# An issue-order edge that keeps a row gather behind the weight splits on VectorE

## Chip, cores and metric

The kernel runs on 1 core of one Trainium2 chip. The metric is the device time of one execution in microseconds. Before the change the median of 3 runs is 3570.77 us (3566.84 to 3582.67 us).

## What is computed

The reference runs two transformer blocks, of depth 2 each, on 256 tokens of width 1024. The change concerns the second block, in which a stream of 256 latent tokens and a stream of 256 context tokens each pass a "PEER" layer: for every token 8 heads choose 16 of 16384 experts, each expert being one row of a table u and one row of a table v.

```
def peer_block(hb, w_q, sub_keys, u_tab, v_tab):
    ...
    expert = jnp.take_along_axis(cand_i, pos, axis=-1)
    g = jax.nn.softmax(top_s, axis=-1)
    u = u_tab[expert]
    act = jax.nn.gelu(jnp.einsum('nhkd,nd->nhk', u, hb).astype(jnp.float32))
    w = (g * act).astype(hb.dtype)
    return jnp.einsum('nhk,nhkd->nd', w, v_tab[expert])
```

## The kernel before, in words

The kernel does not look up rows for most tokens. In its dense form, 448 columns (256 latent tokens, 192 context tokens) go through all 128 slabs of the tables. `ahead` (L1145) computes `hidden` (L1128) for each slab: a 128x1024 piece of u is loaded, split into a high and a low part, multiplied on PE (24 matmuls of 448 columns), put through a GELU and kept in DRAM. `experts` (L1168) then loads each kept slab, weighs it by the routing matrix and multiplies it with a split piece of v. Each split (`split`, L208) is a copy on ACT (L210) and a subtraction on DVE (L211); PE needs both parts. The routing matrix is made beside `ahead`: `choose` (L975) finds the top 16 (DVE, L945 to L949), and `spread` (L1067) builds one-hot tiles (three compares on POOL and one on DVE at L1078, two products on DVE at L1082), multiplies them on PE (L1096) and stores them.

The first 64 context tokens are left out of the dense form. For them `gather` (L1312) fetches the chosen rows: 64 fetches of u rows and 64 of v rows, each 128 rows of 1024 numbers, by an indirect DMA issued on POOL (L1328). Each fetch has one DVE instruction: a product with a sum for u (L1337), a multiply-add for v (L1343; the first one is L1341). There are three landing places, so fetch i+2 needs DVE instruction i-1 to be done. The accumulated result goes to DRAM at the end (L1346, on SP's queue). Two of the three landing places are one tile of the pool "k8", which also holds the split pieces of v.

The source paces this work. `aside` (L1349) ends with `gather` and is a Python generator; each `next` of it traces one fetch and one DVE instruction. Beside the qkv, attention and output projection of the latent stream it is advanced by `beside`. In `ahead` it gets the rate `GP[0]` = 0.22 per unit, and a slab of 448 columns counts two units, so 0.44 gathers per slab. In `experts` it gets `GP[1]` = 0.4 per slab. But the order in which instructions are traced is not the order of the queues: a scheduler sets each engine's queue, and takes first what is ready first.

Of the kernel before, what the change touches and what calls it, by code (L numbers as in the profile page):

```python
# [10 lines left out]
F32 = mybir.dt.float32  # L11
# [3 lines left out]
AF = mybir.ActivationFunctionType  # L15
ALU = mybir.AluOpType
AX = mybir.AxisListType

P = 128
S = 256  # L20
D = 1024
# [37 lines left out]
class Net:  # L59
# [148 lines left out]
    def split(self, hi, lo, src):  # L208

        self.nc.scalar.copy(hi, src)  # L210
        self.nc.vector.tensor_sub(lo, src, hi.bitcast(F32))  # L211

    def cut_in_two(self, shape, raw):

# [1097 lines left out]
    def gather(self, idx, g):  # L1312

        nc, io = self.nc, self.io
        tables = io["u_rows"], io["v"][0].rearrange("a b d -> (a b) d")
        hr, two = self.t("b8", [P, 2, D]), self.t("k8", [P, 2, D])
        h = acc = hr[:, 0]
        places = hr[:, 1], two[:, 0], two[:, 1]  # L1320
        act = self.t("act", [P, P // 2], bufs=1)
        n = P // 2
        for i in range(2):
            nc.sync.dma_start(h[NG * i:NG * i + NG], self.hrd)

        def fetch(i):
            if i < 2 * n:
                nc.gpsimd.indirect_dma_start(out=places[i % 3], out_offset=None, in_=tables[i // n],  # L1328
                                             in_offset=bass.IndirectOffsetOnAxis(ap=idx[:, i % n:i % n + 1], axis=0))

        fetch(0), fetch(1)
        for i in range(2 * n):
            fetch(i + 2)
            r, a = places[i % 3], act[:, i % n:i % n + 1]
            if i < n:
                junk = self.t("b2", [P, D], mybir.dt.bfloat16)
                nc.vector.scalar_tensor_tensor(junk, r, 1.0, h, ALU.mult, ALU.mult, accum_out=a)  # L1337
            elif i == n:
                nc.scalar.activation(act, act, AF.Gelu_apprx_tanh)
                nc.vector.tensor_mul(act, act, g)  # L1340
                nc.vector.tensor_scalar(acc, r, act[:, 0:1], None, ALU.mult)  # L1341
            else:
                nc.vector.scalar_tensor_tensor(acc, r, a, acc, ALU.mult, ALU.add)  # L1343
            yield
        self.accd = self.dr.tile([P, D], F32, tag="accd", name="accd")
        nc.sync.dma_start(self.accd, acc)  # L1346
        yield
# [216 lines left out]
```

## Time and profile before

| | |
|---|---|
| median of 3 runs | 3570.77 us (3566.84 to 3582.67) |
| the profiled execution's own time | 3571.39 us |
| its span in the profile | 3569.5 us |
| mean granted clock of TensorE | 0.974 of full speed |
| busy: PE, DVE, ACT, POOL | 94%, 69%, 42%, 21% of the span |

The stages that the text speaks of, by the time since the span's start: output projection and normalisation of the latent stream about 1110 to 1140 us, key scores from about 1140 us, `ahead` to about 1950 us, `experts` to about 2550 us. The busy share is an average over all stages, so each stage has to be read by itself. In the profile L12 is line 12 of the kernel; a helper's line stands for all its callers, so the weight splits of every stage are L210 and L211. PE executes its queue in order, and so does DVE: an instruction that waits holds back all behind it.

### The profile page before, as it was taken

To read this page: it belongs to the slowest core of one execution; us is meant where nothing else is said; L and a number is where in the kernel's file an instruction comes from. 1 tells how busy PE (TensorE), PEld (TensorE's weight loads), DVE (VectorE), ACT (ScalarE), POOL (GpSimd) and SP (SyncE) were. 2 spreads that over 40 slices of the span, in tenths; PEclk is the share of its full clock that TensorE was granted. 3 is DMA by queue.
4 is the path that set the end of the run, shared out by engine and by line. 5 is a ranking of instruction groups with operands and counts; after the bars stand their busy time and mean duration, and the time that the engine had idled before them with its cause. 6 is when DMAs were issued, how large, how long until landed. Compare 5 with 4: busy or idle time off the path is not lost. (4 is left out here: it accounts for less than half of the span.)

```text
span 3569.5 us, 53463 instructions
## 1 busy us (share of the span) xinstructions
PE 3365.9 (94%) x19488; PEld 2926.8 (82%) x19488; DVE 2445.3 (69%) x5239; ACT 1491.6 (42%) x2523; POOL 743.0 (21%) x728
## 2 busy tenths in 40 slices
PE   8999998999868888899999999999989999999999
PEld 6687867788747867788888999898968999998877
DVE  6657857556878877766666765555467888766665
ACT  6543445444434422233334332333254545555443
POOL 0000001000043476644464000000010046730000
PEclk9999999999988999999999999999999999999999
DMA  7446554344566787754568987787322667788985
GB/s 241 158 159 224 200 168 150 100 153 148 171 204 224 262 272 263 263 186 177 189 219 282 302 266 235 245 256 220 105 67 97 198 239 261 255 287 284 299 277 190
DMA packets 333912, 758.08 MB, mean 212 GB/s; under 512 B 29840, under 2 KB 187920, under 8 KB 327760
## 3 DMA queue, kind: packets, MB, share of 16 engines
q1 hardware_dynamic: 315216, 687.55, 57.3%
q0 software_dynamic: 18432, 67.12, 5.5%
q8 instruction: 153, 2.51, 0.3%
q14 instruction: 111, 0.91, 0.1%
HBM read 659.59 MB, written 94.96 MB: 211 GB/s over the span
## 5 line engine op out<-in xcount | busy, mean ns | idle before, releaser
L210 ACT CAST ws<-w 128x1024 fp32r<-128x1024 f32 (+1 forms) x528 | 547.3, 1037 | 1005.1 <-PE psA L245 728.7
L211 DVE TENSOR_TENSOR ws<-w,ws 128x1024 fp32r<-128x1024 f32 (+1 forms) x528 | 636.6, 1206 | 276.7 <-ACT ws L210 273.7
L246 PE MATMUL psA<-b,ws 128*128 128x256 f32 (+1 forms) x2048 | 669.9, 327 | 50.3 <-DVE ws L211 50.0
L244 PE MATMUL psA<-b,ws 128*128 128x256 f32 (+1 forms) x2048 | 678.5, 331 | 0.0
L1078 POOL TENSOR_SCALAR wb<-iota,R 128x128 f16<-128x128 f16 x528 | 520.6, 1000 | 705.9 <-ACT R L1049 402.7
L245 PE MATMUL psA<-b,ws 128*128 128x256 f32 (+1 forms) x2048 | 665.6, 325 | 0.0
L246 PEld LDWEIGHTS psA<-b,ws 128*128 128x128 f32 x2048 | 390.3, 191 | 78.3 <-DVE ws L211 61.3
L210 ACT CAST k<-wb 128x1024 fp32r<-128x1024 f32 x256 | 268.5, 1051 | 423.8 <-DMA wb<-in_v 423.6
L245 PE MATMUL psC<-k,k 128*128 128x512 f32 (+1 forms) x1056 | 404.9, 384 | 6.1 <-DVE k L211 5.7
L244 PE MATMUL psC<-k,k 128*128 128x512 f32 (+1 forms) x1056 | 402.7, 382 | 6.5 <-ACT k L210 6.5
L246 PE MATMUL psC<-k,k 128*128 128x512 f32 (+1 forms) x1056 | 403.2, 382 | 2.2 <-DVE k L211 2.1
L244 PEld LDWEIGHTS psA<-b,ws 128*128 128x128 f32 x2048 | 392.0, 191 | 15.3
L245 PEld LDWEIGHTS psA<-b,ws 128*128 128x128 f32 x2048 | 390.1, 190 | 15.4
L211 DVE TENSOR_TENSOR k<-wb,k 128x1024 fp32r<-128x1024 f32 x256 | 312.2, 1220 | 68.0 <-ACT k L210 61.5
L159 POOL TENSOR_TENSOR rsrf<-rsvf,neghalf 128x1 f32<-128x1 f32 (+5 forms) x38 | 42.0, 1111 | 1265.8 <-DVE rsvf L158 1264.5
L245 PE MATMUL psC<-ws,k 128*128 128x512 f32 (+1 forms) x608 | 244.0, 401 | 18.0 <-DVE ws L211 17.9
L244 PE MATMUL psC<-ws,k 128*128 128x512 f32 (+1 forms) x608 | 242.0, 403 | 6.6 <-ACT ws L210 5.1
L1191 DVE TENSOR_TENSOR k<-k,b 128x256 f32<-128x256 f32 (+2 forms) x264 | 132.4, 511 | 168.6 <-DMA k<-kept 164.2
L246 PE MATMUL psC<-ws,k 128*128 128x512 f32 (+1 forms) x608 | 241.5, 398 | 0.0
L245 PEld LDWEIGHTS psC<-k,k 128*128 128x128 f32 x1056 | 199.7, 189 | 39.2 <-DVE k L211 8.4
L244 PEld LDWEIGHTS psC<-k,k 128*128 128x128 f32 x1056 | 199.0, 189 | 39.5 <-ACT k L210 7.1
L246 PEld LDWEIGHTS psC<-k,k 128*128 128x128 f32 x1056 | 199.7, 189 | 37.1 <-DVE k L211 5.5
(446 smaller groups left out, 6375.7 us busy)
## 6 DMA issues: line engine op xcount, KB each, us to landing
w<-in_u SPq DMA_DIRECT2D x256, 512.0 KB
wb<-in_v SPq DMA_DIRECT2D x256, 512.0 KB
w<-in_w_ff SPq DMA_DIRECT2D x128, 512.0 KB
G<-k SPq DMA_DIRECT2D x44, 1024.0 KB
wb<-in_ada_w SPq DMA_DIRECT2D x80, 512.0 KB
k<-kept SPq DMA_DIRECT2D x128, 224.0 KB
b<-G SPq DMA_DIRECT2D x15, 1792.0 KB
kept<-k SPq DMA_DIRECT2D x118, 224.0 KB
```

Of the source, the lines that this page charges most:

```text
L159: nc.gpsimd.tensor_tensor(r[:m, :cols], v[:m, :cols], self.neghalf[:m, :cols], op=ALU.pow)
L210: self.nc.scalar.copy(hi, src)
L211: self.nc.vector.tensor_sub(lo, src, hi.bitcast(F32))
L244: self.nc.tensor.matmul(out, ah, bh, start=first, stop=False)
L245: self.nc.tensor.matmul(out, ah, bl, start=False, stop=False)
L246: self.nc.tensor.matmul(out, al, bh, start=False, stop=last)
L1078: eng.tensor_scalar(first[:, j], self.iota16, r0[:, n + j:n + j + 1], None, ALU.is_equal)
L1191: nc.vector.tensor_mul(g3[:, a:b], g3[:, a:b], t[:, :, j])
```

## The change

`split` remembers its DVE subtraction in `self.mark`, and the DVE instructions of one gather step are traced inside `issue_after(self.mark)`. That context gives each DVE instruction in it an ordering edge to the marked one: it is queued behind it on DVE. It is an order of issue alone, with no semaphore. Instructions of other engines are not bound, so neither the indirect DMA on POOL nor the GELU on ACT is.

```
     def split(self, hi, lo, src):
 
         self.nc.scalar.copy(hi, src)
-        self.nc.vector.tensor_sub(lo, src, hi.bitcast(F32))
+        self.mark = self.nc.vector.tensor_sub(lo, src, hi.bitcast(F32)).ins
...
             r, a = places[i % 3], act[:, i % n:i % n + 1]
-            if i < n:
-                junk = self.t("b2", [P, D], mybir.dt.bfloat16)
-                nc.vector.scalar_tensor_tensor(junk, r, 1.0, h, ALU.mult, ALU.mult, accum_out=a)
-            elif i == n:
-                nc.scalar.activation(act, act, AF.Gelu_apprx_tanh)
-                nc.vector.tensor_mul(act, act, g)
-                nc.vector.tensor_scalar(acc, r, act[:, 0:1], None, ALU.mult)
-            else:
-                nc.vector.scalar_tensor_tensor(acc, r, a, acc, ALU.mult, ALU.add)
+            with self.tc.issue_after(self.mark):
+                if i < n:
+                    junk = self.t("b2", [P, D], mybir.dt.bfloat16)
+                    nc.vector.scalar_tensor_tensor(junk, r, 1.0, h, ALU.mult, ALU.mult, accum_out=a)
+                elif i == n:
+                    nc.scalar.activation(act, act, AF.Gelu_apprx_tanh)
+                    nc.vector.tensor_mul(act, act, g)
+                    nc.vector.tensor_scalar(acc, r, act[:, 0:1], None, ALU.mult)
+                else:
+                    nc.vector.scalar_tensor_tensor(acc, r, a, acc, ALU.mult, ALU.add)
```

In the changed kernel the gather's lines are L1338, L1342 and L1344.

Counted over DVE's queue: of the 128 gather instructions, the first 33 stay where they were, give or take some twenty places. Before, the other 95 stand in the normalisation, the key scores and the first third of `ahead`. Now 54 of them stand in `ahead`, 2 or 3 to every 6 weight splits, and 41 in `experts`. The splits, the top-16 search and the one-hots keep their order among one another. Three places follow.

First, DVE's queue in the normalisation after the latent stream's output projection (L174, L158 and L176 are its steps, L941 adds the projection to x, L198 follows PE's transposes), before:

```order
L158 TENSOR_SCALAR rsvf_9979<-nssf_9972 128x1
L1337 SCALAR_TENSOR_TENSOR b_2108_11237,act_8916<-k_1650_8915,b_1649_8914 128x1024
L941 TENSOR_TENSOR x<-x,k_1912_9969 128x512
L176 TENSOR_SCALAR k_1914_9973<-x,rsrf_9980 128x1024
L1337 SCALAR_TENSOR_TENSOR b_2131_11398,act_8916<-b_1649_8914 128x1024
L174 TENSOR_TENSOR nssf_9972<-nssf_9972 128x1
L1337 SCALAR_TENSOR_TENSOR b_2147_11511,act_8916<-k_1650_8915,b_1649_8914 128x1024
L158 TENSOR_SCALAR rsvf_9985<-nssf_9972 128x1
L1337 SCALAR_TENSOR_TENSOR b_2164_11627,act_8916<-k_1650_8915,b_1649_8914 128x1024
L176 TENSOR_SCALAR k_1914_9973<-x,rsrf_9986 128x1024
L1337 SCALAR_TENSOR_TENSOR b_2177_11721,act_8916<-b_1649_8914 128x1024
L198 TENSOR_SCALAR k_1920_9995<-psA_9990,mod_495 128x256
```

And now:

```order
L158 TENSOR_SCALAR rsvf_9979<-nssf_9972 128x1
L941 TENSOR_TENSOR x<-x,k_1912_9969 128x512
L176 TENSOR_SCALAR k_1914_9973<-x,rsrf_9980 128x1024
L174 TENSOR_TENSOR nssf_9972<-nssf_9972 128x1
L158 TENSOR_SCALAR rsvf_9985<-nssf_9972 128x1
L176 TENSOR_SCALAR k_1914_9973<-x,rsrf_9986 128x1024
L198 TENSOR_SCALAR k_1920_9995<-psA_9990,mod_495 128x256
```

The gather instructions between the steps are gone from there.

Second, DVE's queue in `ahead`, at the split whose low part is `ws_12323` (`ws<-w,ws` are the splits of u, `k<-...` at L947 to L949 the top-16 search), before:

```order
L1343 SCALAR_TENSOR_TENSOR b_1649_8914<-k_1650_8915,act_8916,b_1649_8914 128x1024 x2
L947 MATCH_REPLACE k_2254_12237<-k_2235_12128,k_1931_10042 128x128
L211 TENSOR_TENSOR ws_12323<-w_12320,ws_12322 128x1024
L948 MAX k_2235_12128<-k_2254_12237 128x8
L1078 TENSOR_SCALAR wb_12363<-iota_225,R_2239_12145 128x128
L949 MAX_INDEX k_2235_12128<-k_2235_12128,k_2254_12237 128x8
L1082 TENSOR_TENSOR wb_12363<-iota_227,R_12144 128x512
L1343 SCALAR_TENSOR_TENSOR b_1649_8914<-b_1649_8914,act_8916 128x1024
L1082 TENSOR_TENSOR wb_12363<-wb_12363,R_12144 128x512 x2
L1343 SCALAR_TENSOR_TENSOR b_1649_8914<-k_1650_8915,act_8916,b_1649_8914 128x1024
L947 MATCH_REPLACE k_2263_12296<-k_2235_12128,k_1931_10042 128x128
L211 TENSOR_TENSOR ws_12390<-w_12387,ws_12389 128x1024
```

And now:

```order
L947 MATCH_REPLACE k_2254_12237<-k_2235_12128,k_1931_10042 128x128
L211 TENSOR_TENSOR ws_12323<-w_12320,ws_12322 128x1024
L948 MAX k_2235_12128<-k_2254_12237 128x8
L1338 SCALAR_TENSOR_TENSOR b_2271_12355,act_8916<-k_1650_8915,b_1649_8914 128x1024
L949 MAX_INDEX k_2235_12128<-k_2235_12128,k_2254_12237 128x8
L1082 TENSOR_TENSOR wb_12363<-wb_12363,R_12144 128x512 x2
L1078 TENSOR_SCALAR wb_12427<-iota_225,R_2239_12145 128x128
L1082 TENSOR_TENSOR wb_12427<-iota_227,R_12144 128x512
L947 MATCH_REPLACE k_2263_12296<-k_2235_12128,k_1931_10042 128x128
L211 TENSOR_TENSOR ws_12390<-w_12387,ws_12389 128x1024
```

Two gather instructions stood between these two splits and two more before the first; now one stands there, and the next comes two splits later.

Third, DVE's queue in `experts` near the gather's end (`k<-wb,k` is a split of v, `k<-k,k` at L211 a split of the weighed slab, L1191 the weighing), before:

```order
L1191 TENSOR_TENSOR k_3619_21828<-k_3619_21828,b_3590_21577 128x448
L211 TENSOR_TENSOR k_3602_21659<-k_3599_21651,k_3602_21659 128x448
L211 TENSOR_TENSOR k_3609_21726<-wb_21724,k_3609_21726 128x1024
L211 TENSOR_TENSOR k_3606_21695<-k_3603_21687,k_3606_21695 128x448
L211 TENSOR_TENSOR k_3613_21761<-wb_21759,k_3613_21761 128x1024
```

And now:

```order
L1191 TENSOR_TENSOR k_3619_21828<-k_3619_21828,b_3590_21577 128x448
L211 TENSOR_TENSOR k_3602_21659<-k_3599_21651,k_3602_21659 128x448
L1344 SCALAR_TENSOR_TENSOR b_1649_8914<-b_1649_8914,act_8916 128x1024
L211 TENSOR_TENSOR k_3605_21691<-wb_21689,k_3605_21691 128x1024
L211 TENSOR_TENSOR k_3606_21695<-k_3603_21687,k_3606_21695 128x448
L211 TENSOR_TENSOR k_3609_21726<-wb_21724,k_3609_21726 128x1024
```

There was no gather here before. While the gather lives, the split of v (`k_3609`) also stands one slab later against the split of the weighed slab (`k_3606`) than it did.

## Rows read from the trace of the kernel before

**Rows 1.** The page, parts 1 and 3: busy engines; the queue of the indirect DMAs.
```profile
PE 3365.9 (94%) x19488; PEld 2926.8 (82%) x19488; DVE 2445.3 (69%) x5239; ACT 1491.6 (42%) x2523; POOL 743.0 (21%) x728
...
q0 software_dynamic: 18432, 67.12, 5.5%
```
**Rows 2.** Windows by stage: length; busy us of PE, PEld, DVE, ACT, POOL; clock; DMA, GB/s.
```profile
1110.00:1140.00 30.00, 18.63 (x81) 15.21 (x81) 25.64 (x46) 9.61 (x19) 12.84 (x11) 0.73 0.84 298
1140.00:1240.00 100.00, 89.88 (x671) 85.71 (x670) 83.53 (x249) 40.71 (x70) 37.15 (x25) 0.94 0.71 243
1240.00:1500.00 260.00, 218.72 (x1162) 188.98 (x1161) 207.00 (x470) 74.26 (x114) 178.49 (x154) 0.93 0.79 270
1500.00:1800.00 300.00, 300.00 (x1727) 267.68 (x1725) 191.58 (x552) 113.07 (x170) 129.41 (x138) 1.00 0.52 187
1800.00:1950.00 150.00, 145.77 (x877) 129.17 (x876) 96.60 (x193) 60.26 (x92) 94.91 (x96) 0.99 0.73 250
1950.00:2550.00 600.00, 590.82 (x2870) 539.93 (x2871) 360.57 (x514) 191.76 (x250) 0.00 (x0) 0.99 0.77 247
```
**Rows 3.** Windows of L211 alone: DVE busy (weight splits), clock, DMA.
```profile
1240.00:1500.00 260.00, 46.64 (x38) 0.93 0.79 270
1500.00:1800.00 300.00, 68.04 (x56) 1.00 0.52 187
```
**Rows 4.** Waits of PE, 1240 to 1500 us: total, times, longest.
```profile
PE psA L246 <- DVE ws L211: 41.4, 18, 6.8
```
**Rows 5.** Waits of DVE, 1240 to 1500 us.
```profile
DVE b L1343 <- DMA k<-in_v,idx: 27.1, 18, 4.3
DVE b L1343 <- DMA b<-in_v,idx: 22.4, 9, 5.0
```
**Rows 6.** Windows of L1343 alone: DVE busy in the gather.
```profile
1240.00:1500.00 260.00, 81.85 (x63) 0.93 0.79 270
```
**Rows 7.** Timeline of DVE at one stall in `ahead`: start, us, instruction, idle before.
```profile
1401.52 1.28 DVE L1343 SCALAR_TENSOR_TENSOR b<-b,act 128x1024 f32<-128x1024 f32 x1 [4.14 <-DMA b<-in_v,idx]
...
1405.09 1.22 DVE L211 TENSOR_TENSOR ws<-w,ws 128x1024 fp32r<-128x1024 f32 x1
```
**Rows 8.** Timeline of PE at the same stall.
```profile
1406.36 0.74 PE L246 MATMUL psA<-b,ws 128*128 128x448 f32 x1 [3.29 <-DVE ws L211]
1406.90 0.57 PE L244 MATMUL psA<-b,ws 128*128 128x448 f32 x1
1407.27 0.57 PE L245 MATMUL psA<-b,ws 128*128 128x448 f32 x1
...
1412.57 0.37 PE L245 MATMUL psA<-b,ws 128*128 128x448 f32 x1
1412.78 0.37 PE L246 MATMUL psA<-b,ws 128*128 128x448 f32 x1
```
**Rows 9.** Waits of PE, 1110 to 1240 us.
```profile
PE psA L246 <- DVE ws L211: 7.8, 6, 2.7
PE psA L186 <- DVE k L176: 6.1, 1, 6.1
```
**Rows 10.** Windows of L1337 alone, in the normalisation: DVE busy.
```profile
1120.00:1136.00 16.00, 8.62 (x14) 0.67 0.77 261
```
**Rows 11.** Windows of L1078 alone: DVE busy, POOL busy (one-hot compares).
```profile
1240.00:1500.00 260.00, 7.82 (x30) 92.04 (x90) 0.93 0.79 270
1500.00:1800.00 300.00, 12.43 (x46) 129.41 (x138) 1.00 0.52 187
```
**Rows 12.** L1328 (the fetches), 1240 to 1500 us: what POOL waited for; issue to landing.
```profile
  DVE b L1343: 45.9, 17
...
DMA to landing us min/median/max: 5.3/6.3/10.9
```
**Rows 13.** Window in `experts`; and a wait of DVE, 1950 to 2550 us.
```profile
2000.00:2050.00 50.00, 50.00 (x247) 45.91 (x246) 37.67 (x57) 17.33 (x22) 0.00 (x0) 1.00 0.96 307
...
DVE b L778 <- DMA wb<-in_ada_w: 101.7, 34, 10.9
```

## The prediction

> **What bounds the kernel now.** I read the page first, then windows by stage, then the waits of PE and DVE in the stage where PE has gaps, and last two timelines at one gap.
>
> PE is busy 94% of the span, DVE 69% [rows 1]. That average hides two regimes. From 1500 to 1800 us `ahead` runs with PE busy all 300 us at a granted clock of 1.00; from 1240 to 1500 us, in the same loop, PE is busy 218.7 of 260 us, at 0.93 [rows 2]. Both have the same work per slab: 38 weight splits in the 260 us and 56 in the 300 us [rows 3], so 6.84 us and 5.36 us for each; the one-hot compares on POOL are 90 and 138 [rows 11], 2.4 and 2.5 per split. What differs is the gather: 63 of its multiply-adds stand in the slow stretch and none in the fast one.
>
> What ends last there is DVE. PE waits 41.4 us for the low part of a split and for nothing else of size [rows 4]. DVE is busy 207.0 us [rows 2], of which 81.9 are the gather [rows 6], and it idles 49.5 us before gather instructions whose rows have not landed [rows 5]. Together that is 256.5 of 260 us: DVE is full, half of it with the gather. One gap shows it: DVE waits 4.14 us for a fetch, the split queued behind starts at 1405.09 [rows 7], and PE idles 3.29 us until 1406.36; then PE's matmuls start 0.37 us apart until 1412, where they go back to 0.21 [rows 8]. That is PE's clock at its lower level (1.2 GHz) after the gap; some 15 matmuls at 0.16 us each more are 2.4 us on top of the idle time.
>
> **The change, part by part.** Nothing is added or removed: the same 128 fetches and 128 DVE instructions, no semaphore. 95 gather instructions move later on DVE, and their fetches with them on POOL, since a fetch needs the instruction three before.
>
> *In `ahead`, 1240 to 1500 us.* 63 gather instructions for 38 slabs become 0.42 per slab (54 in 128), so a DVE load of (207.0 - 81.9) / 38 = 3.29 us plus 0.42 x 1.30 (81.85 / 63, rows 6) = 0.55, or 3.84 us per slab. The fast stretch has 191.6 / 56 = 3.42 us of DVE work per slab [rows 2, 3] and PE is full there at 5.36 us. So PE sets the pace again: 38 x (6.84 - 5.36) = **56 us gained**. The other way of counting agrees: 41.3 us of PE idle time plus 7% of 219 us for the clock are 57.
>
> The waits for rows should go too. Now a gather comes every 4 us and a fetch lands after 5.3 to 10.9 us [rows 12]; then it comes every 12 us (5.36 / 0.44), with two fetches under way. If the waits stayed whole (49.5 / 63 = 0.8 us each), they would still meet a DVE with 1.5 us to spare per slab.
>
> *Key scores, 1140 to 1240 us.* PE idles 10.1 us and loses 6% of 89.9 us to the clock [rows 2]: 15.5 us at most, 0 at least, since the gather instructions leave this stretch altogether but only 7.8 us of the waits between 1110 and 1240 are named as waits for a split [rows 9]. I take 10, nearer the upper end because the rest of the idle time has no other named cause.
>
> *Normalisation, 1110 to 1140 us.* Seven gather instructions stand between its steps and take 8.6 us [rows 10]; PE waits 6.1 us for the scaled x [rows 9]. Bounds: 0 (the chain over ACT and POOL is as long) and 16 (11.4 us idle plus 27% of 18.6 us, rows 2). I take 6, the named wait.
>
> *What the later places cost.* In the fast part of `ahead`, 0.55 us more DVE work per slab lies beside 1.9 us of DVE idle time: nothing, unless that cover is gone. It is thinnest from 1800 to 1950 us, where PE already idles 4.2 us and POOL is 63% busy with one-hots; 12 fetches there, one every 12 us, at (178.5 - 92.0) / 63 = 1.4 us of POOL time each [rows 2, 6, 11] make it 74%. I take a second 4 us. In `experts`, 41 gathers of 1.3 us lie beside DVE's 239 us of idle time [rows 2]. Their transfers, 41 x 0.524 MB (67.12 MB / 128, rows 1), add 36 GB/s to 247 and by 5.5% of the span / 128 = 1.53 us each some 63 us of DMA time, 0.77 to 0.88 of the engines; another window shows 0.96 and 307 GB/s with PE full [rows 13]. What can suffer is the reserve before PE: the split of v stands a slab later, its pool being short of the gather's tile, and DVE still meets waits of up to 10.9 us for another load [rows 13]. Bounds: 0, and 41 x 0.88 = 36 us, the price of a gather now (56 / 64); I take 8, nearest to PE's present 9.2 us of idle time there.
>
> *Edits at nothing.* The first 33 gathers keep their stretch. The GELU on ACT and the final store on SP move with the gather; the store waits for the last instruction, but the next v load behind it on SP needs a buffer that DVE frees one instruction later, so it loses nothing.
>
> Sum against the profiled execution, 3571.4 us (0.6 above the median, so no correction): -56 - 10 - 6 + 4 + 8 = -60, **3511 us**.
>
> **A rule that speaks against it.** The mean compare on POOL is 92.04 / 90 = 1.02 us beside the gather and 129.41 / 138 = 0.94 without [rows 11], 0.08 us apart. The Trainium skill, page "SBUF — State Buffer", section "SBUF: two separate sides", says that DVE and GpSimd share a pair of ports under an exclusive lock: a DVE instruction with two SBUF inputs makes a GpSimd instruction that reads SBUF wait for its whole length. By the rows the cost is within the 4 us above; by that rule each moved gather could hold a compare, as in the second rival.
>
> **The rivals.** One bound for all: a measurement of this kernel can tell about 0.5%, 18 us, from no change, so faster means under 3553 and slower over 3589.
>
> 1. *The price of a gather stays.* If each of the 95 still costs PE what it costs now, 0.88 us, the 84 us eat the 72 gained and the time is 3583; at half that price, 3541. For it: DVE is in order, and every wait still holds a split. Against: the price came with DVE full. Chance 0.11, half for each value.
> 2. *Ports.* Each of 54 gathers in `ahead` holds one compare for its 1.3 us. POOL has idle time for it except at the end, where 12 gathers would cost 16 us: 3527. For it: POOL's 1.02 against 0.94 us. Against: 0.08 us is a small part of 1.3. Chance 0.08.
> 3. *Transfers bound `experts`.* If DMA were the limit there in effect, 21.5 MB at 247 GB/s add 87 us in place of my 8: 3590. For it: a DMA share of 0.77 and DVE waits for loads. Against: 307 GB/s with PE full. Chance 0.03.
> 4. *POOL stalls in front of fetches (slower).* The fetch is not bound by the edge but waits for a DVE instruction that now stands behind a split, and the one-hot compares for PE queue behind it on POOL. POOL's waits for the gather are 45.9 us in 17 now [rows 12], 2.7 us each; if all 54 in `ahead` passed such a wait on to PE, 146 us would be added to 3571 - 72 + 8: 3653. It decides from 64 / 54 = 1.2 us per gather. Against: POOL idles 57% of the fast stretch, and what PE waits for in the slow one is splits [rows 4]. Chance 0.04.
> 5. *Nothing happens.* The edge binds order only, and a queue might have come out the same; the queues above show that it did not. 0.02, at 3571.
>
> **How the numbers follow.** The forecast has 0.72, with its own range 3483 (the upper bounds 56 + 16 + 16 and no cost) to 3540. Faster: 0.72 + 0.08 + 0.055 = 0.85; within 0.5%: 0.055 + 0.02 = 0.08; slower: 0.04 + 0.03 = 0.07. The range goes from 3482 to 3552, which takes in rival 2 and half of rival 1 and leaves out 0.15.
>
> **What would show it.** Right: about 13 to 17 gather instructions where 63 stood in 260 us, no row "PE waits for the split" of tens of us in `ahead`, a split every 5.4 us from its start, PE's clock at 1.00, and hardly any DVE wait for fetched rows. Normalisation: no gather between L174 and L176, PE's wait for L176 shorter. Wrong: PE idle in `experts` of tens of us with waits for v splits or kept slabs (rival 3, or a larger reserve lost), POOL waits for the gather together with PE waits for one-hots (rival 4), or slabs at 6 us and more in all of `ahead` (rival 1).

## Result and profile after the change

The changed kernel takes 3521.82 us, median of 4 runs (3515.7 to 3527.85), against 3574.07 us in 4 runs of the kernel before (3566.84 to 3582.67): ratio 0.9853, 95% interval 0.9823 to 0.9883. Forecast were 3511 us, 3482 to 3552: the sign and the range held, and the gain of 52 us is 8 us short of the 60 predicted. The profiled execution of the changed kernel is its slowest, 3527.85 us.

First its page, part 1, the busy engines:

```profile
PE 3355.5 (95%) x19488; PEld 2918.0 (83%) x19488; DVE 2438.3 (69%) x5239; ACT 1490.5 (42%) x2523; POOL 764.2 (22%) x728
```

The work is that of [rows 1]. The windows by stage, with the columns of [rows 2]:

```profile
1110.00:1140.00 30.00, 20.14 (x84) 16.11 (x83) 20.10 (x37) 10.40 (x20) 7.92 (x8) 0.83 0.65 227
1140.00:1240.00 100.00, 99.70 (x772) 95.71 (x771) 70.34 (x236) 46.18 (x78) 12.93 (x12) 1.00 0.54 181
1240.00:1500.00 260.00, 260.00 (x1493) 232.03 (x1492) 190.26 (x540) 99.09 (x148) 155.91 (x143) 1.00 0.66 224
1500.00:1800.00 300.00, 294.54 (x1719) 261.25 (x1718) 221.81 (x568) 109.83 (x170) 193.78 (x182) 1.00 0.68 234
1800.00:1950.00 150.00, 134.69 (x727) 120.19 (x726) 106.31 (x175) 57.18 (x79) 54.37 (x51) 0.94 0.91 313
1950.00:2550.00 600.00, 582.06 (x2832) 529.23 (x2830) 370.99 (x508) 180.96 (x251) 51.91 (x33) 0.99 0.74 246
```

From 1140 to 1500 us PE is now full at a clock of 1.00, where it was busy 89.88 of 100 and 218.72 of 260 us. In `experts` it is busy less than before (582.06 against 590.82 us), and the window from 1800 to 1950, which holds the border between the loops, is at 0.94. A window by the clock compares stages that have moved, so the rest of the text counts by stages. Their borders are the first and last starts of a line; for `ahead`, as an example, the GELU on a slab (L1142) and the transposes behind `experts` (L1398, now L1399). The rows of those lines end in duration (min/median/max ns) and first and last start, before:

```profile
L1142 ACT ACTIVATE k<-psA x128: 372/539/551, 1210.0 to 1949.3; 128x448 f32<-128x448 f32 x118, 128x256 f32<-128x256 f32 x10
...
L1398 PE MATMUL psC<-c_ident,k x32: 272/272/331, 2578.3 to 2596.9; 128*128 128x128 f32 x32
```

and after:

```profile
L1142 ACT ACTIVATE k<-psA x128: 372/539/568, 1200.5 to 1876.3; 128x448 f32<-128x448 f32 x118, 128x256 f32<-128x256 f32 x10
...
L1399 PE MATMUL psC<-c_ident,k x32: 272/272/328, 2530.1 to 2548.7; 128*128 128x128 f32 x32
```

So from the last GELU of `ahead` to the transposes it was 2578.3 - 1949.3 = 629.0 us and is 653.8. All profiled executions in that way, in us (the kernels below these two are explained under Experiments; an "SP edge" is an edge on SP, the engine whose queue issues the loads and stores): "start" to the first L186 of the second block, "attention" to the first L941, "norm" to the last L186, "keys" to the last L970, `ahead` to the last L1142, `experts` to the transposes, "end" to the end of the span.

| kernel | start | attention | norm | keys | `ahead` | `experts` | end |
|---|---|---|---|---|---|---|---|
| before | 993.8 | 118.9 | 27.8 | 64.0 | 744.8 | 629.0 | 991.2 |
| changed | 1000.2 | 119.7 | 19.8 | 56.6 | 680.0 | 653.8 | 995.7 |
| no fetches (before) | 991.5 | 108.6 | 22.0 | 58.1 | 675.0 | 628.9 | 995.4 |
| no late fetches | 1002.7 | 119.3 | 19.9 | 56.5 | 680.7 | 628.3 | 993.2 |
| edge on v alone | 993.9 | 117.3 | 28.9 | 64.0 | 692.7 | 656.4 | 992.8 |
| edge on u alone | 994.1 | 117.4 | 21.1 | 56.5 | 738.2 | 622.5 | 995.9 |
| rate 0.4 | 994.4 | 115.4 | 20.1 | 56.6 | 684.8 | 625.5 | 996.1 |
| two SP edges | 1000.1 | 119.5 | 19.9 | 56.5 | 678.3 | 652.8 | 995.7 |
| rate 0.4, two SP edges | 1003.1 | 118.9 | 20.0 | 56.6 | 686.9 | 620.7 | 993.6 |
| one SP edge | 1001.5 | 117.4 | 21.3 | 56.8 | 681.4 | 647.3 | 990.1 |
| no late fetches, two SP edges | 992.1 | 115.9 | 19.8 | 56.6 | 679.1 | 621.5 | 988.6 |
| rate 0.5 | 993.2 | 117.0 | 21.2 | 56.6 | 674.0 | 626.5 | 993.8 |
| rate 0.6 | 994.0 | 117.6 | 20.8 | 56.5 | 678.6 | 623.8 | 996.6 |
| rate 0.83 | 1003.7 | 118.3 | 20.7 | 56.6 | 720.8 | 626.0 | 995.9 |

In "start" and "end" all kernels run the same work, and these still differ by up to 12 and 8 us. The change is thus -8.0 in the norm, -7.4 in the keys, -64.8 in `ahead` and **+24.8 in `experts`**, -55.4 us together; the other three stages add 11.7 in these two executions, which is within what they differ by anyway.

Two places in the changed kernel tell how. In `ahead` PE has no wait at all from 1240 to 1500 us, and DVE's waits for rows from 1110 to 1500 us, 49.5 us in [rows 5] alone, are down to two:

```profile
DVE b L1338 <- DMA k<-in_u_rows,idx: 4.2, 1, 4.2
DVE b L1338 <- DMA b<-in_u_rows,idx: 1.7, 1, 1.7
```

The gather still stands there, 22 instructions (of two records each) where 63 stood [rows 6], and 48 splits where 38 stood [rows 3]:

```profile
1240.00:1500.00 260.00, 26.83 (x44) 1.00 0.66 224
...
1240.00:1500.00 260.00, 59.06 (x48) 1.00 0.66 224
```

(L1338 alone, then L211 alone.) In `experts` PE waits for split slabs, as its waits from 1890 to 2490 us show:

```profile
PE psC L245 <- DVE k L211: 16.7, 12, 2.9
PE psC L244 <- ACT k L210: 13.2, 1, 13.2
```

Before, from 1950 to 2550 us, these two were:

```profile
PE psC L245 <- DVE k L211: 5.7, 3, 3.0
PE psC L244 <- ACT k L210: 3.1, 1, 3.1
```

The 13.2 us are one gap, at the border. SP's timeline shows what stands ahead of the first kept slab there (start, us that the issue took, instruction):

```profile
1863.81 4.92 SPq L119 DMA_DIRECT2D w<-in_w_qkv  x2
...
1876.39 0.59 SPq L1184 DMA_DIRECT2D b<-G  x1
1877.04 8.50 SPq L1154 DMA_DIRECT2D kept<-k  x1
1885.58 1.40 SPq L119 DMA_DIRECT2D k<-kept  x3
```

SP was held 8.50 us at the last store of a kept slab, and the loads of kept slabs queue behind it. New ahead of it are the third routing load of `experts` (1.8 MB, `b<-G`) and a fifth weight load of the next layer: the scheduler has moved them up. Before, the first kept load and then this store came ahead of both, and the store took 0.33 us:

```profile
1945.53 0.42 SPq L119 DMA_DIRECT2D k<-kept  x1
1949.84 0.33 SPq L1154 DMA_DIRECT2D kept<-k  x1
```

### The profile page after: what moved, and what is told of

It is laid out like the page before. It is cut to its first block, busy times and chain, and to the rows that moved or that the text cites. A ratio compares the mean times of both kernels' runs of the same rounds, so it can differ in the third digit from the quotient of the medians.

```text
span 3525.8 us, 53411 instructions
## 1 busy us (share of the span) xinstructions
PE 3355.5 (95%) x19488; PEld 2918.0 (83%) x19488; DVE 2438.3 (69%) x5239; ACT 1490.5 (42%) x2523; POOL 764.2 (22%) x728
## 5 line engine op out<-in xcount | busy, mean ns | idle before, releaser
L211 DVE TENSOR_TENSOR ws<-w,ws 128x1024 fp32r<-128x1024 f32 (+1 forms) x528 | 637.5, 1208 | 298.8 <-ACT ws L210 296.5
L1078 POOL TENSOR_SCALAR wb<-iota,R 128x128 f16<-128x128 f16 x528 | 546.1, 1048 | 639.8 <-ACT R L1049 402.8
L244 PE MATMUL psA<-b,ws 128*128 128x256 f32 (+1 forms) x2048 | 671.7, 328 | 0.0
L246 PE MATMUL psA<-b,ws 128*128 128x256 f32 (+1 forms) x2048 | 659.5, 322 | 2.3 <-DVE ws L211 2.0
L245 PE MATMUL psA<-b,ws 128*128 128x256 f32 (+1 forms) x2048 | 658.7, 322 | 0.0
L246 PEld LDWEIGHTS psA<-b,ws 128*128 128x128 f32 x2048 | 384.7, 188 | 21.8 <-DVE ws L211 5.1
L244 PEld LDWEIGHTS psA<-b,ws 128*128 128x128 f32 x2048 | 386.0, 188 | 15.1
L245 PEld LDWEIGHTS psA<-b,ws 128*128 128x128 f32 x2048 | 384.8, 188 | 14.8
L211 DVE TENSOR_TENSOR k<-wb,k 128x1024 fp32r<-128x1024 f32 x256 | 312.2, 1220 | 110.7 <-ACT k L210 110.4
L1191 DVE TENSOR_TENSOR k<-k,b 128x256 f32<-128x256 f32 (+2 forms) x264 | 131.8, 511 | 195.0 <-DMA k<-kept 188.9
```

Of the source, the lines that this page charges most:

```text
L211: self.mark = self.nc.vector.tensor_sub(lo, src, hi.bitcast(F32)).ins
L244: self.nc.tensor.matmul(out, ah, bh, start=first, stop=False)
L245: self.nc.tensor.matmul(out, ah, bl, start=False, stop=False)
L246: self.nc.tensor.matmul(out, al, bh, start=False, stop=last)
L1078: eng.tensor_scalar(first[:, j], self.iota16, r0[:, n + j:n + j + 1], None, ALU.is_equal)
L1191: nc.vector.tensor_mul(g3[:, a:b], g3[:, a:b], t[:, :, j])
```

## Experiments

The question of the first four runs: is a gather's price in `ahead` the wait for its rows, or DVE's time; and what costs 25 us in `experts`?

**No fetches.** The kernel before, with only the first three of the 128 fetches made (`fetch`, L1327). DVE's 128 instructions stay, at nearly their old places in its queue, and work on what lies in the landing places:

```
-            if i < 2 * n:
+            if i < 3:
```

> The kernel before, with only the first three of the 128 indirect fetches made; the 128 gather instructions on DVE stay, at nearly the same places, and work on whatever lies in the landing places. It takes the waits for rows and the fetches' traffic away and leaves DVE's busy time. Theory A (DVE in ahead is full only together with its waits for rows): 207 us of DVE work for 38 slabs is 5.45 us each, next to PE's 5.36, so most of the 56 us come back, with some of the normalisation: about 3520 us. Rival (the gather's busy time on DVE is the price, the waits only stand beside it): 82 of the 131 us stay, so about 35 of the 56 us stay: about 3553 us.

Measured: 3483.86 us (3475.04 to 3489.55), ratio 0.9749, 0.9713 to 0.9784. Its window from 1240 to 1500 us:

```profile
1240.00:1500.00 260.00, 258.69 (x1478) 230.14 (x1477) 230.38 (x557) 95.88 (x143) 150.41 (x118) 1.00 0.52 183
```

DVE is busier than before, 230.38 of 260 us, with 52 gather instructions beside 48 splits, and PE is full. So the price was not the instructions. The run takes away the waits for rows and with them the fetches' transfers and their issue on POOL; of these only the waits stood in front of the splits that PE waited for [rows 4, 5]. By stages it gains 69.8 in `ahead`, 10.3 in attention and 11.7 in norm and keys, and the gain is more than the expected 3520 us since waits before `ahead` go too. This kernel is a mark for the others: it shows what the fetches cost in all.

**No late fetches.** The changed kernel, with `if i < 89:` in the same place, which leaves out the last 39 fetches.

> The changed kernel, with the fetches from number 89 on left out (all that fall into experts); the gather instructions on DVE stay where they are. In the changed kernel the stretch from the last hidden slab to the end of experts is 25 us longer than before, where the prediction had 8. Theory T (the transfers added to a stage at a DMA share of 0.77 to 0.96 delay the kept slabs and v): about 20 us come back, about 3500 us, and the PE gap of 13 us at the start of experts shrinks. Rival D (DVE's added work, or the order of SP's queue, that the edge changed): no difference, about 3522 us, the gap stays.

Measured: 3497.87 us (3492.32 to 3505.88), ratio 0.9786, 0.9751 to 0.9822; `experts` takes 628.3 us, as before the change. Its window of `experts`:

```profile
1900.00:2500.00 600.00, 600.00 (x2937) 550.49 (x2936) 408.72 (x545) 190.37 (x247) 0.00 (x0) 1.00 0.75 241
```

DVE's order, with the gather instructions among the splits and the v split one slab later, is that of the changed kernel, and PE does not wait once. So the waits of 16.7 us come from the late transfers and not from DVE's work or order. The way leads over the kept slabs, for which DVE waits longer beside these transfers. In the changed kernel, then without the late fetches, from 1900 to 2500 us:

```profile
DVE k L1191 <- DMA k<-kept: 118.5, 62, 8.4
```
```profile
DVE k L1191 <- DMA k<-kept: 87.9, 58, 3.5
```

The gap at the border stays (11.3 us), which theory T did not expect: the late fetches are not its cause.

**The edge on half of the gather.** On v's instructions alone (i >= n), then on u's alone (i < n):

```
-            with self.tc.issue_after(self.mark):
+            with self.tc.issue_after(self.mark) if i >= n else ExitStack():
```

> The changed kernel with the edge for the second half of the gather alone (the multiply-adds of v rows). The first half stands as before: 31 products move back into the normalisation and the key scores. By the forecast's terms the 16 us of these two stretches are lost again and ahead keeps its gain: about 3537 us. Rival (the hoisted first half costs nothing, the gain is all in ahead): about 3522 us.

> The changed kernel with the edge for the first half of the gather alone. The second half is free again: its 64 multiply-adds stand in the last third of ahead (89 to 119 of 128 within 15 splits), none in experts. Theory A: DVE is full again there, 3.3 + 1.4 x 1.3 + waits is about 6.3 us for 45 slabs in place of 5.4, 41 us lost, but the 20 us in experts come back: about 3543 us. Rival (only the normalisation and the key scores mattered, or the start of ahead with its top-16 search): about 3500 us.

Measured: v alone 3549.93 us (ratio 0.994, 0.992 to 0.996), u alone 3549.13 (0.994, 0.9916 to 0.9964). Windows of v alone:

```profile
1140.00:1240.00 100.00, 89.02 (x668) 85.20 (x666) 81.85 (x246) 40.44 (x70) 35.84 (x26) 0.94 0.70 239
1240.00:1500.00 260.00, 259.09 (x1490) 231.76 (x1491) 170.97 (x515) 98.11 (x148) 114.99 (x122) 1.00 0.54 190
```

and of u alone:

```profile
1140.00:1240.00 100.00, 99.70 (x764) 95.34 (x763) 71.42 (x244) 46.13 (x77) 18.26 (x17) 1.00 0.59 192
1240.00:1500.00 260.00, 260.00 (x1487) 232.20 (x1486) 192.60 (x541) 98.18 (x147) 156.53 (x144) 1.00 0.68 227
```

The edge on v pays in `ahead` (-52.1 by the table) and costs in `experts` (+27.4); the edge on u pays in norm and keys (-14.2). With v alone the time is 13 us above the 3537 expected: the 16 us of norm and keys are lost as forecast, but `ahead` also gains 12.7 us less than with the whole edge. With u alone the v gathers crowd together again once the last u is done, only later, and their waits with them, from 1500 to 1930 us:

```profile
DVE b L1344 <- DMA k<-in_v,idx: 37.4, 15, 6.0
...
DVE b L1344 <- DMA b<-in_v,idx: 14.9, 8, 3.7
```

PE waits for splits there:

```profile
PE psA L246 <- DVE ws L211: 32.5, 12, 5.9
```

So `ahead` gains 6.6 instead of 64.8 us: both halves of the edge are needed, and a crowd later in `ahead` costs PE as the earlier one did.

**Where the late fetches could go, and the gap.** If `ahead` has room for all of the gather, nothing need fall into `experts`. The rate in `ahead` is a constant:

```
-GP = (0.22, 0.4)
+GP = (0.4, 0.4)
```

> The changed kernel with the gather's rate in `ahead` at 0.4 instead of 0.22 per unit (0.8 instead of 0.44 steps per slab): all 128 steps end within `ahead`, none falls into `experts`. Nothing is left out. Theory T (what the changed kernel loses in `experts` is the transfers of the 41 late fetches, 24 us by the run without them, and `ahead` has room for them because PE is full there and DVE is busy 73%): `experts` from 1900 us on has PE busy all the time, `ahead` stays near 676 us, about 3500 us. Rival P (a gather step in `ahead` costs PE again as soon as they come twice as densely, by waits for rows as in the kernel before): `ahead` grows by 20 us or more and `experts` shrinks by as much, about 3520 us, no better than the change. Rival D (the loss in `experts` is the split of v that stands one slab later while the gather holds its tiles, and not the transfers): `experts` also gets faster here, and this run alone doesn't tell D from T, but the run without the late fetches kept those DVE instructions and gained 24 us, which is against D.

Measured: 3500.57 us (3494.8 to 3507.86), ratio 0.9808, 0.9784 to 0.9832, as theory T has it. `experts` takes 625.5 us. `ahead` takes 4.8 us more than in the changed kernel, and not for rows: PE's waits from 1720 to 1860 us are for one-hots on POOL, which has its fetches to issue as well:

```profile
PE psC L1096 <- POOL wb L1078: 10.2, 11, 2.1
```

For the gap, the routing loads of the second step on and the next layer's weight loads got an edge behind the first kept load (`self.seen`, taken from the last load traced before). Both edges:

```
-                for t, a, b in Gs:
-                    nc.sync.dma_start(t, Gd[:, a:b, m * c:m * c + m])
+                with self.tc.issue_after(self.seen) if c and N > S else ExitStack():
+                    for t, a, b in Gs:
+                        nc.sync.dma_start(t, Gd[:, a:b, m * c:m * c + m])
...
-        qT, kT, v, kTc, vc = self.done(self.qkv(fg, 1, hT, True, hc))
+        with self.tc.issue_after(self.seen):
+            qT, kT, v, kTc, vc = self.done(self.qkv(fg, 1, hT, True, hc))
```

> The changed kernel with two more ordering edges on SP's queue: the routing-matrix loads of the second and later steps of `experts`, and the next layer's qkv weight loads, are issued behind the first load of a kept slab. Nothing is left out. Theory Q (the 13 us gap of PE at the start of `experts` comes from SP's queue: in the changed kernel five weight loads and a 1.8 MB routing load stand ahead of the first kept load, before the change they stood behind it): the gap shrinks to about 3 us as in the kernel before, about 3512 us. Rival S (the first kept load waits for the last kept store and the DMA engines, wherever it stands; the gap is the DMA rate at that moment): the gap stays above 9 us, 3517 to 3527 us, the same as the change.

and the first of them alone:

> Of the two SP edges only the one on the routing-matrix loads; the five qkv weight loads still stand ahead of the first kept load. Nothing is left out. Theory Q has two candidates for what holds the first kept load: if the 1.8 MB routing load is it, the gap at the start of `experts` shrinks here as with both edges (about 3512 us); if the weight loads are it (5 x 0.26 to 0.5 MB, two of which took 4.92 us to be issued), the gap stays near 13 us and the time near 3522 us.

and both edges with rate 0.4:

> The two edits together: all gather steps within `ahead`, and the first kept load ahead of the other loads. If T and Q both hold: 3522 - 24 - 10 = about 3488 us, near the 3484 us of the kernel without the fetches. If the two mend the same microseconds: about 3500 us. If P and S hold: about 3520 us.

Measured: both edges 3521.4 us (ratio 0.9855, 0.9828 to 0.9882), one edge 3521.88 (0.9865, 0.9829 to 0.99), both with rate 0.4 3500.44 (0.9801, 0.9779 to 0.9823). The gap shrinks to 3.6 us with both edges and to 5.2 with one, so SP's order made it, as theory Q says, and the routing load does most of it. But no time is gained. With both edges PE's waits from 1890 to 2500 us are

```profile
PE psC L245 <- DVE k L211: 21.8, 15, 4.2
```

instead of 16.7: the start of `experts` is paid later. Theory Q has the gap right and its price wrong; with rate 0.4 SP's queue has the third routing load behind the first kept loads anyway and the gap is short (4.6 us), so the edges bring nothing more. What a gap costs without late transfers, the last run asked: no late fetches and both edges.

> The run without the late fetches (it leaves out the last 39 of the 128 fetches, so these rows are not gathered) together with the two edges on SP's queue that closed the gap at the start of `experts` from 13.2 to 3.6 us. Alone the first gave 3498 us with a gap of 11.3 us, alone the second changed nothing (3521 against 3522 us). If the gap had a price of its own, which in the second run the late transfers ate up again: 3498 - 8 = about 3490 us. If transfers queued at that moment have to be paid anyway, at the start or a little later: 3494 to 3502 us, with waits of PE for the weighed slab that the run without late fetches does not have.

Measured: 3478.2 us (3475.42 to 3485.56), ratio 0.9755, 0.9732 to 0.9778, against 0.9786 without the edges; the intervals overlap. By stages `experts` goes from 628.3 to 621.5 us with the gap from 11.3 to 3.6, and PE has no other wait. So the gap has a price of its own of some 7 us, and in the changed kernel the late transfers eat it up. The total fell by 19.7 us, to 12 below the 3490 expected, but 10.6 us of that stand in "start", where both kernels run the same work.

**How dense may the gather stand?** Three more rates, the same edit with 0.5, 0.6 and 0.83:

> The changed kernel with the gather's rate at 0.5 per unit, 1.0 step per slab (0.44 in the change, 0.8 in the run at 0.4, about 1.66 in the slow stretch of the kernel before). DVE work per slab by rows of the kernel before: 3.42 + 1.0 x 1.30 = 4.7 of PE's 5.36 us, so PE still sets the pace. The last step comes near 1710 us, so POOL's last one-hots stand without fetches beside them: theory E (the 12 us that PE lost between 1720 and 1840 us at 0.4 were fetches on POOL in front of one-hots) expects `ahead` some 5 us shorter than there, about 3495 us. Rival P (the waits for rows come back with density): PE waits for splits between 1240 and 1700 us, above 3505 us.

> The changed kernel with the gather's rate at 0.6 per unit, 1.2 steps per slab, between the run at 0.5 (1.0 step, 3487 us, no wait for rows between 1200 and 1500 us) and the run at 0.83 (1.66 steps, 3530 us, 34 us of DVE waits for rows there). DVE work per slab: 3.42 + 1.2 x 1.30 = 5.0 of PE's 5.36 us; the fetches ask for 1.2 x 0.524 MB in 5.36 us. Theory A1 (the price begins where DVE has no room left, at (5.36 - 3.42) / 1.30 = 1.5 steps per slab) expects PE full from 1240 to 1500 us and 3483 to 3490 us. Rival A2 (it begins earlier, where a step comes faster than a fetch lands through three places, so that waits for rows hold splits although DVE has room): waits of PE for splits of 10 us and more, above 3497 us.

> The changed kernel with the gather's rate at 0.83 per unit: 1.66 steps per slab, as many as the kernel before had in its slow stretch, but each behind a split and none before `ahead`. DVE work per slab: 3.42 + 1.66 x 1.30 = 5.6 us, just above PE's 5.36 us. Theory A (the price of a gather is the wait for its rows at that density, since three landing places can't bring them faster) expects the price back: 95 steps in 57 slabs, of which each costs PE up to 0.88 us, less the 0.2 us x 57 that DVE alone would cost: 3500 + 40 to 80 = 3540 to 3580 us, with waits of DVE for rows of 30 us and more and waits of PE for splits. Rival O (what cost the time was the order in which the scheduler put the gather instructions, several in a row in front of a split, and not their number) expects no more than DVE's own excess, 57 x 0.25 = 14 us: about 3510 us.

Measured: 0.5: **3486.8 us** (3484.19 to 3490.32), ratio 0.9747, 0.9731 to 0.9763. 0.6: 3490.52 (0.9762, 0.9728 to 0.9795). 0.83: 3530.02 (0.9858, 0.9842 to 0.9875). Their windows from 1240 to 1500 us, in this order:

```profile
1240.00:1500.00 260.00, 260.00 (x1486) 232.18 (x1486) 223.10 (x563) 97.79 (x146) 198.06 (x169) 1.00 0.84 279
```
```profile
1240.00:1500.00 260.00, 259.89 (x1485) 231.64 (x1484) 235.00 (x570) 98.31 (x148) 215.54 (x179) 1.00 0.87 298
```
```profile
1240.00:1500.00 260.00, 237.57 (x1299) 206.89 (x1298) 228.20 (x547) 86.27 (x130) 196.06 (x172) 0.97 0.88 300
```

Up to 1.2 steps per slab PE is full with DVE busy 235 of 260 us. At 1.66 the old picture is back, although every gather instruction stands behind a split. DVE's largest waits for rows at that rate, from 1200 to 1500 us, and what PE waited for from 1240 us on:

```profile
DVE b L1344 <- DMA k<-in_v,idx: 13.2, 12, 2.8
DVE b L1338 <- DMA k<-in_u_rows,idx: 8.9, 4, 5.4
DVE b L1344 <- DMA b<-in_v,idx: 7.1, 6, 3.3
```
```profile
PE psA L246 <- DVE ws L211: 22.4, 13, 5.0
```

`ahead` is 46.8 us longer than at 0.5, in the 40 to 80 us of theory A; the total came out below its 3540 because the base was 3487 and not 3500. Rival O's 14 us are too few. The run at 0.6 has the full PE of theory A1, and half a microsecond more than its 3490; rival A2's waits of PE for splits did not come. But A1's reason, that DVE has no room left from 1.5 steps per slab on, is not the limit. The run without fetches shows 1.7 steps per slab from 1240 to 1400 us, with DVE busy all the time and PE full beside it (all instructions, then L1343 and L211 alone):

```profile
1240.00:1400.00 160.00, 158.69 (x904) 141.14 (x903) 159.46 (x357) 58.32 (x88) 101.45 (x72) 1.00 0.51 178
1240.00:1400.00 160.00, 64.27 (x50) 1.00 0.51 178
1240.00:1400.00 160.00, 35.09 (x29) 1.00 0.51 178
```

So what costs is a density at which the steps wait for rows; it begins between 1.2 and 1.66 steps per slab. An estimate agrees: from 1240 to 1500 us a step came every 3.7 us at 1.66 (260 / 71) and every 4.5 us at 1.2 (260 / 58), and with three landing places a fetch has less than three steps, 11 and 13 us, to be issued and to land. The landing alone took up to 11.8 us at 1.66 and up to 9.4 us at 1.2. That the number of places sets the limit is not shown, since no run has another number. The edge helps by making the density that of the source. Without it the rate is a dead letter: built with a rate of 0.5, but not timed, the kernel before gets the same sequence of instructions on DVE as with 0.22. Theory E holds too: at 0.5 the last gather instruction starts at 1694 us, PE's waits for one-hots behind 1500 us are 3.2 us instead of 10.2, and `ahead` is 10.8 us shorter than at 0.4, where some 5 were expected.

The version with rate 0.5 beats both kernels: 2.5% under the kernel before, 35 us under the change. It lies 3 us from the run without fetches, which is within the spread of either, and in `ahead` nothing is left of the fetches' price (674.0 against 675.0 us).

## Why the prediction was right, and where it was off

The mechanism that it forecast was right: the waits for rows and for splits in `ahead` are gone, and PE is full there. That the sum came so near, -55.4 by stages against -60, is in part luck. The stretches before `experts` gained 12 us more than forecast, and `experts` lost 17 us more.

- *`ahead`, 1240 to 1500 us, -56*: right. 48 splits in 260 us are 5.42 us each, 38 x (6.84 - 5.42) = 54. The waits went as forecast. But the reason given was too wide: "DVE is full, half of it with the gather". The run without fetches has the same gather instructions and a DVE busy 230 us, and PE full. Of the two parts of that sum, the waits for rows decided.
- *Key scores, 1140 to 1240 us, -10*: too small. The window went from 89.88 us at 0.94 to 99.70 at 1.00, which is the upper bound, 15. By stages the key scores hold 7.4 of it; the rest is the first 36 us of `ahead`, which lie in that window and paid like the rest of `ahead`.
- *Normalisation, -6*: -8.0.
- *The thin end of `ahead`, +4*: +3.2. PE idled 449 - 445.25 = 3.75 us from 1500 us to the last GELU before, and 376 - 369.03 = 6.97 after; it waits for one-hots, as the prediction has it.
- *`experts`, +8*: this is **the step that failed**, by its size: +24.8. The bounds were 0 and 36, and the value was taken "nearest to PE's present 9.2 us of idle time". The two dangers named were the transfers and the reserve of v splits. It was the transfers: without them and with the same DVE order `experts` is back at 628.3 us. 38 fetches are issued from 1870 us on, 25.5 / 38 = 0.67 us each, not 0.2. The window of 0.96 and 307 GB/s with PE full [rows 13] was 50 us long, and it did not stand for the loop: in the changed kernel from 1900 to 2500 us PE is busy only 583.25 of 600 us at a DMA share of 0.82 and 271 GB/s. That the short window lived on a reserve of loaded slabs is a guess; no run shows it. The change of SP's order at the border was not foreseen at all; it made a gap of 13 us, whose price is inside the 24.8.

Rival 1 (the price of a gather stays) fell in `ahead` and holds for `experts`, where a late fetch costs 0.67 of the 0.88 us. Rival 3 (transfers bound `experts`) is the same effect at a third of its 87 us. Rival 4 did not come: POOL waits for gather instructions in both loops, and PE behind it has no wait from 1240 to 1500 us:

```profile
  DVE b L1338: 33.8, 9
...
DMA to landing us min/median/max: 4.1/4.7/6.1
```

(L1328 in the changed kernel, 1240 to 1500 us; the landing was 5.3/6.3/10.9 in [rows 12].)

Rival 2 (ports) cannot be told by time, but the compares on POOL did get longer. L1078 alone, in the changed kernel:

```profile
1240.00:1500.00 260.00, 11.03 (x41) 131.88 (x121) 1.00 0.66 224
1500.00:1800.00 300.00, 14.33 (x51) 167.22 (x159) 1.00 0.68 234
```

That is 1.09 and 1.05 us each, where the stretch without a gather had 0.94 [rows 11]; in the run without fetches, where 230 of 260 us of DVE are busy, it is 1.27 (150.41 / 118 on POOL, from 1240 to 1500 us). The 280 compares took 36 us more than at 0.94. The Trainium skill, page "SBUF — State Buffer", section "SBUF: two separate sides", has a GpSimd instruction that reads SBUF wait for the end of a DVE instruction with two SBUF inputs that started first; the direction agrees, the size is about half of 54 x 1.3 us. PE paid the 3.2 us above for it and for the fetches together, because POOL had the idle time.

## What to carry over

A paced instruction that a scheduler may pull forward needs an edge to the work that it is paced against; only then does the rate in the source set the density, and the rate then has to be chosen anew (here 0.5 instead of 0.22 was worth as much again as two thirds of the edge). Price such a fetch by its density, from the wait for its data, and not by its engine's busy time. When work is moved off one loop into another, sum up the DMA time that it brings there over the whole loop, since a short window with a full engine may live on a reserve.

## What was not expected of the hardware

- A full DVE beside a full PE: 235 of 260 us busy and PE 259.89 at a clock of 1.00 (rate 0.6); without fetches even 159.46 of 160 us, with PE at 158.69. A load of 90% is no bound by itself.
- The issue of a DMA on SP can take 8.50 us where 0.33 us is usual, at a DMA share of 0.95 and 321 GB/s (1840 to 1900 us), and all that SP has queued waits for it.
- Closing a gap of 10 us of PE moved the total by nothing (3521.4 against 3521.8 us), as long as the late fetches were there; without them it moved `experts` by 7 us.
- Stretches that run the same work in all kernels differed by up to 12 us from one profiled execution to the next (991.5 to 1003.7 us), more than some of the effects sought; only counting by stages showed those.
